# Six small softmax tiles move from a phase's pool to a pool in front of it

## The chip, the cores and the metric

The kernel runs on one core of a Trainium2 chip. The metric is the device time of one execution in microseconds (us). Before the change, three runs gave 1282.92, 1283.75 and 1287.06 us, so the median is 1283.75 us. All inputs and the output are float32.

## The reference: what is computed

Two layers work on 256 latent tokens of width 1024; 256 context tokens go through the first layer's first half as well. Each layer is half-step SwiGLU, token mixer, half-step SwiGLU; the mixer is neighbourhood attention in layer 0 and a short gated convolution in layer 1. Every sub-layer ends in a post-norm update.

```python
def swiglu_ffn(h, w_in, w_out):
    a, u = jnp.split(h @ w_in, 2, axis=-1)          # w_in: 1024 x 5632, w_out: 2816 x 1024
    return (jax.nn.silu(a) * u) @ w_out

def post_norm_update(x, y, gate, res_w, g, b):
    return layer_norm(DN_ALPHA * x + res_w * gate * y, g, b)

x <- post_norm_update(x, f(x * (1 + scale) + shift), gate, w, g, b)   # f: FFN, attention or convolution
```

In the attention each of 16 heads takes a softmax over 256 latent keys (with a bias and a window mask) and 256 context keys. shift, scale and gate come from a product of the conditioning vector with a 1024 x 9216 matrix per layer ("ada").

## The kernel before, in words

**Products.** A float32 product is made of three matmuls on rounded parts: a weight chunk is split into `hi` (ScalarE, L179) and `lo = raw - hi` (VectorE, L182), the activations likewise, and TensorE adds hi by hi, hi by lo and lo by hi into one bank of PSUM (L157, L158, L160 in the helper `mmu`; L549 to L551 in the first FFN, where the weights are the stationary operand and the 512 tokens the moving one). Elsewhere a 128x128 piece of the activations is stationary and 512 columns of the weights are moving. So every such matmul reads two places of SBUF: 128 columns that are loaded as weights, and 512 columns that stream.

**Weight units.** `wunit` (L163 to L183) brings in 128 x 1024 floats (two chunks of 128 rows by 512 columns) by DMA into a `raw` tile and splits it into an `hi` and an `lo` tile. Of these, most come from the pool `wp` (five `hi` and five `lo` buffers). Some come from the pool `hp` of the phase that is running:

```python
        if ext[0] and ext[1] % (5 + ext[0]) in (E0 if ext[0] == 1 else E2):
            hi = hp.tile([P, UN], F32R, tag="whx", bufs=ext[0], name=nm(s + "h"))
            lo = hp.tile([P, UN], F32R, tag="wlx", bufs=ext[0], name=nm(s + "l"))
        else:
            hi = wp.tile([P, UN], F32R, tag="wh", bufs=WB[1], name=nm(s + "h"))
```

In the first phase that is every sixth unit (11 in all, with one extra buffer), in the second phase none, and in the third phase three of every eight (87 in all, with three extra buffers). A unit in the third phase serves 12 matmuls: two tiles of 128 tokens, two chunks, three matmuls. The 11 of the first phase serve 24 each.

**Phases and pools.** SBUF is given out in the order in which pools are opened: `cp` (constants), `wp` (weights), `ap` (38 activation tiles), `sp` (small tiles and scratch), and behind them the pool of the running phase. `ph0` lives through the context tokens' FFN and the latent one's, `ph1` through the attention, `ph2` through the rest; each starts where `sp` ends. `ph0` and `ph2` hold, beside the extra weight buffers, the ada rows (`ar`), their accumulators (`acc`), a few rows more, and in `ph0` the context tokens (`xc`). `ph1` holds `bias` and `kr`, then the six `mx` tiles, then `pr`, `pT` and `oT`.

**Order.** The order on TensorE is written out by hand (a manual schedule, which the helpers `panels`, `tile_panel` and `out_gemm` walk through); a scheduler orders the other engines by priorities. `panels` goes through an FFN's first product in panels of 512 columns: 4 units, 48 matmuls; four units' worth of steps after a panel is done, TensorE transposes its gated result with 8 short matmuls (L408), so a stretch of 48 large matmuls lies between two groups of transposes.

**The softmax.** `scores` (L812 to L834) makes two heads' scores in two PSUM banks, adds the bias, takes the row maximum into `mx[:, 0:1]`, the exponentials with their sum into `mx[:, 1:2]`, and the reciprocal into `mx[:, 2:3]`.

Of the kernel before, what the change touches and what calls it, by code (L numbers as in the profile page):

```python
# [9 lines left out]
F32 = mybir.dt.float32  # L10
# [6 lines left out]
P = 128  # L17
# [48 lines left out]
def backbone_kernel(  # L66
# [11 lines left out]
    sp = ctx.enter_context(tc.tile_pool(name="sp", bufs=2))  # L78
# [3 lines left out]
    hp = phase.__enter__()  # L82
# [6 lines left out]
    def nm(s):  # L89
        uid[0] += 1  # L90
        return f"{s}_{uid[0]}"
# [4 lines left out]
    def bank(tag, s):  # L96
        return pp.tile([P, 512], F32, tag=tag, bufs=PB[tag], name=nm(s))
# [714 lines left out]
    def scores(h, qt):  # L812

        ch = h % 8 // 2
        qh, ql = Q[h // 8].get()[ch // 2]
        qs = slice((ch % 2) * 256 + qt * P, (ch % 2) * 256 + (qt + 1) * P)
        kh, kl = KV[h // 4][0].get()[(h % 4) // 2]
        banks = [bank("at", "S") for _ in range(2)]
        for f in range(3):
            for i in range(2):  # L820
                ps = slice(64 * i, 64 * i + 64)
                nc.tensor.matmul(banks[i], (qh, qh, ql)[f][ps, qs], (kh, kl, kh)[f][ps, :], start=f == 0, stop=f == 2)
        res = []
        for i, S in enumerate(banks):
            Sv = S[:, 0:256].rearrange("p (a b) -> p a b", a=4)
            nc.vector.tensor_tensor(out=Sv, in0=Sv, in1=BIAS.pop((h + i, qt)), op=ALU.add)
            mx = hp.tile([P, 3], F32, tag="mx", bufs=6, name=nm("mx"))
            nc.vector.tensor_reduce(out=mx[:, 0:1], in_=S, axis=AX.X, op=ALU.max, negate=True)
            pr = hp.tile([P, 512], F32, tag="pr", bufs=4, name=nm("pr"))
            nc.scalar.activation(pr, S, AF.Exp, bias=mx[:, 0:1], accum_out=mx[:, 1:2])  # L830
            nc.vector.reciprocal(mx[:, 2:3], mx[:, 1:2])
            nc.scalar.activation(pr, pr, AF.Copy, scale=mx[:, 2:3])
            res.append(pr)
        return res  # L834
# [39 lines left out]
    hp = phase.__enter__()  # L874
# [35 lines left out]
    for i in range(len(steps) + LAG + V_LAG):  # L910
        if i == NX_AT:
            new_x(0, 0, s2t)
            for t in range(2):
                for h in range(2):
                    sync.dma_start(xscr[t * P:(t + 1) * P, h * 512:(h + 1) * 512], xt[t][h])
        while i + AHEAD < len(steps) and len(KV) <= steps[i + AHEAD][0] // 4:
            fill_some(1)
        if i < len(steps) and i % 2 == 0:
            with tc.high_priority(offset=S_EARLY):
                prs[i], prs[i + 1] = scores(*steps[i])  # L920
            if i % 2 == 0 and i + 2 < len(steps):
                bias_pair(*steps[i + 2])
        credit += rate[min(i, len(rate) - 1)]
        n = int(credit)
        credit -= n
        if i >= 24 and fin is None:
            run(fill)
            fin = last_filler()
            fill = islice(fin, 9)
        fill_some((n + 1) // 2)  # L930
        if 0 <= i - LAG < len(steps):
            with tc.high_priority(offset=P_EARLY):
                probs_T(*steps[i - LAG], prs.pop(i - LAG))
        fill_some(n // 2)
        j = i - LAG - V_LAG
        if j >= 0 and steps[j][1] == 1:
            with tc.high_priority(offset=V_EARLY):
                values(steps[j][0])
# [5 lines left out]
    hp = phase.__enter__()  # L944
# [126 lines left out]
```

## Time and profile before

| what | value |
|---|---|
| median of three runs | 1283.75 us |
| the profiled execution's own time | 1283.45 us |
| its span, from first to last instruction | 1281.7 us |
| mean granted TensorE clock | 0.997 |
| TensorE (PE) busy | 1255.1 us, 98% |
| weight loads (PEld) busy | 1005.4 us, 78% |
| VectorE (DVE) busy | 954.6 us, 74% |
| ScalarE (ACT) busy | 591.2 us, 46% |
| DMA | 268.59 MB, mean 210 GB/s |

The page names each group of instructions by its line, its engine and its tiles (`w<-w1h,hTh` is a matmul that writes `w` from the tiles `w1h` and `hTh`). A matmul's listed duration covers the part of its run that overlaps the next one, so durations of matmuls add up to more than the time; how fast TensorE goes is read from the distance between the starts of two matmuls that follow each other. In a table by windows the columns are: the stretch, its length, the engine's busy time in it with the count of instructions that reach into it in brackets, the granted clock, the DMA engines' busy share, GB/s.

### The profile page before, as it was taken

The numbers are of one execution on the slowest core, as the hardware profiler recorded it, in microseconds if no ns is written. First come the engines' busy times: TensorE is split into PE (matmuls) and PEld (weight loads), VectorE is DVE, ScalarE is ACT, GpSimd is POOL, SyncE is SP. The second block draws the span as 40 slices with busy tenths as digits, with TensorE's granted clock in tenths as the row PEclk, the third lists the DMA queues.
The fourth block names the chain that finished last, engine by engine and source line by source line (L and its number), as shares of the span: only waits on it lengthen the run. The fifth ranks groups of instructions, "written<-read, shape, count | busy, mean of one in ns | idle before, by whom it ended". The sixth has DMA issues, their size and how long they took to land.

```text
span 1281.7 us, 17190 instructions
## 1 busy us (share of the span) xinstructions
PE 1255.1 (98%) x5890; PEld 1005.4 (78%) x5890; DVE 954.6 (74%) x1683; ACT 591.2 (46%) x1148; POOL 42.7 (3%) x71
## 2 busy tenths in 40 slices
PE   7999999999999999988999999999999999999997
PEld 4787778788778777766787787887788877788886
DVE  3699878495658777788998788867778787865545
ACT  2432132413236456686556435655435744655431
POOL 0000000000001111120000000000000000000000
PEclk9999999999999999999999999999999999999999
DMA  9977569394622744464999887777886754776641
GB/s 291 301 232 238 181 194 307 123 306 133 204 71 83 216 91 91 92 149 133 307 336 313 307 289 271 233 225 228 290 285 221 247 194 131 226 220 188 229 154 51
DMA packets 202713, 268.59 MB, mean 210 GB/s; under 512 B 30027, under 2 KB 149299, under 8 KB 202625
## 3 DMA queue, kind: packets, MB, share of 16 engines
q1 hardware_dynamic: 202624, 267.49, 65.8%
q8 instruction: 46, 0.75, 0.2%
q14 instruction: 43, 0.34, 0.1%
HBM read 265.27 MB, written 2.17 MB: 209 GB/s over the span
## 4 chain that ended last, share of the span: by engine, by line
PE 87%; DVE 5%; DMA 3%; ACT 3%; issue 1%; POOL 0%; SPq 0%; DVEq 0%; ACTq 0%
PE w L157 16%; PE w L158 16%; PE w L160 16%; PE f L549 6%; PE f L550 6%; PE f L551 6%; PE wkv L157 2%; DMA w1r<-in_ffn_w_in_dram 2%; PE wkv L158 2%; PE wkv L160 2%; PE wc L157 2%; PE wc L158 2%; PE wc L160 2%; DMA ar<-in_ada_w_dram 2%; PE gT L408 1%
## 5 line engine op out<-in xcount | busy, mean ns | idle before, releaser
L179 ACT ACTIVATE w1h<-w1r 128x512 fp32r<-128x512 f32 x352 | 202.6, 625 | 181.4 <-PE w L160 68.8
L182 DVE TENSOR_TENSOR w1l<-w1r,w1h 128x512 fp32r<-128x512 f32 x352 | 227.8, 687 | 65.9 <-ACT w1h L179 63.5
L157 PE MATMUL w<-w1h,hTh 128*128 128x512 f32 x528 | 210.8, 399 | 1.4 <-ACT hTh L106 1.4
L248 DVE SCALAR_TENSOR_TENSOR acc<-ar,cst,acc 128x512 f32<-128x512 f32 x266 | 187.5, 749 | 29.4 <-DMA ar<-in_ada_w_dram 29.4
L158 PE MATMUL w<-w1l,hTh 128*128 128x512 f32 x528 | 207.0, 392 | 0.0
L157 PE MATMUL w<-w2h,gh 128*128 128x512 f32 (+1 forms) x446 | 175.4, 394 | 0.0
L158 PE MATMUL w<-w2l,gh 128*128 128x512 f32 (+1 forms) x446 | 173.6, 390 | 0.0
L179 ACT ACTIVATE w2h<-w2r 128x512 fp32r<-128x512 f32 x176 | 101.5, 624 | 140.2 <-PE w L160 129.4
L160 PE MATMUL w<-w1h,hTl 128*128 128x512 f32 x528 | 163.5, 391 | 0.7 <-DVE hTl L107 0.6
L182 DVE TENSOR_TENSOR w2l<-w2r,w2h 128x512 fp32r<-128x512 f32 x176 | 114.2, 688 | 43.9 <-ACT w2h L179 42.6
L549 PE MATMUL f<-h0h,w1h 128*128 128x512 f32 x352 | 139.6, 396 | 0.4 <-ACT w1h L179 0.4
L551 PE MATMUL f<-h0l,w1h 128*128 128x512 f32 x352 | 138.2, 393 | 0.0
L550 PE MATMUL f<-h0h,w1l 128*128 128x512 f32 x352 | 138.2, 393 | 0.0
L160 PE MATMUL w<-w2h,gl 128*128 128x512 f32 (+1 forms) x446 | 136.3, 387 | 0.0
L157 PEld LDWEIGHTS w<-w1h,hTh 128*128 128x128 f32 x528 | 99.2, 188 | 25.4 <-ACT hTh L106 2.7
L160 PEld LDWEIGHTS w<-w1h,hTl 128*128 128x128 f32 x528 | 98.9, 188 | 24.2 <-DVE hTl L107 1.9
L158 PEld LDWEIGHTS w<-w1l,hTh 128*128 128x128 f32 x528 | 99.2, 188 | 20.4 <-DVE w1l L182 0.3
L157 PEld LDWEIGHTS w<-w2h,gh 128*128 128x128 f32 x446 | 83.8, 188 | 21.7 <-issue 1.7
L160 PEld LDWEIGHTS w<-w2h,gl 128*128 128x128 f32 x446 | 83.3, 188 | 18.8
L158 PEld LDWEIGHTS w<-w2l,gh 128*128 128x128 f32 x446 | 83.7, 188 | 18.0 <-DVE w2l L182 0.7
L549 PEld LDWEIGHTS f<-h0h,w1h 128*128 128x128 f32 x352 | 66.4, 189 | 18.3 <-issue 3.8
L551 PEld LDWEIGHTS f<-h0l,w1h 128*128 128x128 f32 x352 | 66.3, 188 | 14.7 <-DVE h0l L527 0.3
(178 smaller groups left out, 1703.1 us busy)
## 6 DMA issues: line engine op xcount, KB each, us to landing
w1r<-in_ffn_w_in_dram SPq DMA_DIRECT2D x352, 256.0 KB
ar<-in_ada_w_dram SPq DMA_DIRECT2D x128, 512.0 KB
w2r<-in_ffn_w_out_dram SPq DMA_DIRECT2D x88, 512.0 KB
ar<-in_ada_w_dram SPq DMA_DIRECT2D x32, 256.0 KB
wkvr<-in_na_w_qkv_dram SPq DMA_DIRECT2D x32, 256.0 KB
wcr<-in_sc_w_in_dram SPq DMA_DIRECT2D x32, 256.0 KB
wqr<-in_na_w_qkv_dram SPq DMA_DIRECT2D x8, 512.0 KB
bias<-in_na_rpb_dram SPq DMA_DIRECT2D x64, 64.0 KB
```

The lines of the kernel that those rows point to most:

```text
L157: nc.tensor.matmul(ps, lh, rh, start=first and i == 0, stop=False)
L158: nc.tensor.matmul(ps, lh, rl, start=False, stop=False)
L160: nc.tensor.matmul(ps, ll, rh, start=False, stop=last and i == n - 1)
L179: nc.scalar.activation(hi[:, a:a + m // W_HI], raw[:, a:a + m // W_HI], AF.Copy)
L182: nc.vector.tensor_tensor(out=lo[:, a:b], in0=raw[:, a:b], in1=hi[:, a:b].bitcast(F32), op=ALU.subtract)
L248: nc.vector.scalar_tensor_tensor(out=a, in0=src, scalar=sc, in1=a, op0=ALU.mult, op1=ALU.add)
L408: nc.tensor.transpose(ps[:, j * 256 + i * P:j * 256 + (i + 1) * P], g[:, j * P:(j + 1) * P], ident)
L549: nc.tensor.matmul(ps, lh, hT0[k][0], start=(k == 0), stop=False)
L550: nc.tensor.matmul(ps, ll, hT0[k][0], start=False, stop=False)
L551: nc.tensor.matmul(ps, lh, hT0[k][1], start=False, stop=(k == KC - 1))
```

## The change

The six `mx` tiles (128 x 3 floats, 32 bytes of each partition apiece, 192 bytes together) are taken from `sp` and no longer from the phase's pool.

```diff
@@ -824,7 +824,7 @@
         for i, S in enumerate(banks):
             Sv = S[:, 0:256].rearrange("p (a b) -> p a b", a=4)
             nc.vector.tensor_tensor(out=Sv, in0=Sv, in1=BIAS.pop((h + i, qt)), op=ALU.add)
-            mx = hp.tile([P, 3], F32, tag="mx", bufs=6, name=nm("mx"))
+            mx = sp.tile([P, 3], F32, tag="mx", bufs=6, name=nm("mx"))
             nc.vector.tensor_reduce(out=mx[:, 0:1], in_=S, axis=AX.X, op=ALU.max, negate=True)
             pr = hp.tile([P, 512], F32, tag="pr", bufs=4, name=nm("pr"))
             nc.scalar.activation(pr, S, AF.Exp, bias=mx[:, 0:1], accum_out=mx[:, 1:2])
```

The two built programs hold the same instructions in the same order on every engine, with the same semaphores and the same waits. They differ in the addresses of 458 tiles and in nothing else. These are the byte addresses within a partition of the tiles that matter here, and what is left of them when divided by 512:

| tiles | before: address, remainder | after: address, remainder |
|---|---|---|
| weight units in `wp` (`hi`, `lo`) | 38208 + n x 4096 and 58688 + n x 4096: 320 | the same |
| activations in `ap` (38 tiles of 2048) | 79168 + n x 2048: 320 | the same |
| scratch of 2048 in `sp` | 156992 + n x 2048: 320 | the same |
| `mx`, six tiles of 32 | 192128 to 192288 | 179840 to 180000 |
| weight units in `ph0` | 216704, 220800: 128 | 216896, 220992: 320 |
| weight units in `ph2` | 179840 + n x 4096, 192128 + n x 4096: 128 | 180032 + n x 4096, 192320 + n x 4096: 320 |
| `ar`, `acc`, rows, `xc`, gates in `ph0` and `ph2` | remainder 128 | remainder 320 |
| `bias`, `kr` in `ph1` (ahead of `mx`) | remainder 128 | remainder 320 |
| `pr`, `pT`, `oT` in `ph1` (behind `mx`) | 192320 to 229176: 320 | the same |

A chunk within a tile starts a multiple of 512 bytes further on, so each tile keeps one remainder throughout.

## The prediction

> **What bounds the kernel now.** I read the page's busy times and chain of waits first.
>
> ```profile
> PE 1255.1 (98%) x5890; PEld 1005.4 (78%) x5890; DVE 954.6 (74%) x1683; ACT 591.2 (46%) x1148; POOL 42.7 (3%) x71
> ...
> PE 87%; DVE 5%; DMA 3%; ACT 3%; issue 1%; POOL 0%; SPq 0%; DVEq 0%; ACTq 0%
> ```
>
> TensorE sets the end, so any nanosecond per matmul counts some 4,900 times. The next view is that of the waits, of TensorE and then of ScalarE.
>
> ```profile
> PE ada L502 <- DMA ar<-in_ada_w_dram: 5.0, 5, 1.6
> ...
> PE w L157 <- ACT hTh L106: 1.4, 3, 0.6
> ...
> PE f L549 <- ACT w1h L179: 0.4, 1, 0.4
> ...
> ACT w2h L179 <- PE w L160: 129.4, 59, 17.3
> ...
> ACT w1h L179 <- PE w L160: 68.8, 50, 16.7
> ...
> ACT w1h L179 <- DMA w1r<-in_ffn_w_in_dram: 51.7, 34, 5.5
> ```
>
> TensorE waits for nothing for long (5.0 us is its longest entry, all at the start). ScalarE, which makes the weights' `hi` tiles, waits 198 us for TensorE to free a buffer and 52 us for weights to land: the supply is ahead.
>
> So the question is how fast TensorE goes where it waits for nothing. That is read from the starts in the timeline of PE. Here is a stretch of the first FFN; the first six matmuls use a unit of `wp`, the six from 193.87 on the one unit of `ph0`, those after 195.27 units of `wp` again (the program's order tells which).
>
> ```profile
> 192.51 0.39 PE L549 MATMUL f<-h0h,w1h 128*128 128x512 f32 x1
> 192.74 0.39 PE L550 MATMUL f<-h0h,w1l 128*128 128x512 f32 x1
> ...
> 193.87 0.40 PE L549 MATMUL f<-h0h,w1h 128*128 128x512 f32 x1
> 194.10 0.39 PE L550 MATMUL f<-h0h,w1l 128*128 128x512 f32 x1
> 194.34 0.40 PE L551 MATMUL f<-h0l,w1h 128*128 128x512 f32 x1
> ...
> 195.27 0.39 PE L549 MATMUL f<-h0h,w1h 128*128 128x512 f32 x1
> ...
> 196.66 0.39 PE L549 MATMUL f<-h0h,w1h 128*128 128x512 f32 x1
> ```
>
> From 192.51 to 193.87 are six steps: 1.36 us, 226.7 ns each. From 193.87 to 195.27, with the phase's unit: 1.40 us, 233 ns. From 195.27 to 196.66, back on `wp`: 1.39 us, 232 ns. Nothing waits; TensorE is simply slower while one of its operands lies in a tile of remainder 128, and for about six matmuls after it.
>
> The same shows in whole panels of the last FFN. Of every eight units three lie in `ph2`; the transposes cut these so that in one stretch 5 of 47 matmuls use them and in the next 30.
>
> ```profile
> 1114.30:1124.76 10.46, 10.46 (x47) 1.00 0.51 156
> 1125.66:1136.26 10.60, 10.60 (x47) 1.00 0.77 244
> 1137.17:1147.63 10.46, 10.46 (x47) 1.00 0.57 176
> 1148.53:1159.13 10.60, 10.60 (x48) 1.00 0.58 177
> 1160.03:1170.51 10.48, 10.48 (x48) 1.00 0.58 175
> 1171.41:1182.01 10.60, 10.60 (x48) 1.00 0.59 174
> ```
>
> Each window holds 46 steps. 10.46 us is 227.4 ns a step, 10.60 is 230.4 ns. The clock is full in all six and the DMA share 0.57 to 0.59 in four of them, so neither makes the difference; 25 matmuls more on phase tiles cost 0.14 us.
>
> **Is it the remainder, or the place high up in SBUF?** The attention's output product answers: there the stationary operand `oT` lies at 217408 to 228672, as high as the phase's weight units, but behind `mx` and so at remainder 320.
>
> ```profile
> 592.63 0.39 PE L157 MATMUL wo<-woh,oT 128*128 128x512 f32 x1
> ...
> 593.53 0.39 PE L157 MATMUL wo<-woh,oT 128*128 128x512 f32 x1
> ...
> 596.71 0.39 PE L157 MATMUL wo<-woh,oT 128*128 128x512 f32 x1
> ```
>
> At 593.53 the stationary operand goes from `ap` (146752) to `ph1` (217408). The 18 steps from 592.63 to 596.71 take 4.08 us, 226.7 ns each, with no break at the crossing. Distance in SBUF costs nothing; what the slow steps share is two operands of different remainder.
>
> **The change part by part.** Nothing is added or removed, and the order of instructions is the same on every engine, so there is no new wait to cost. Three things change their address.
>
> *The weight units of the phases*, 98 units, 1,308 matmuls (87 x 12 and 11 x 24), go to remainder 320, that of all other operands of the large matmuls. I took the windows of all 43 stretches of at least 37 large matmuls without a break.
>
> ```profile
> 49.10:99.50 50.40, 50.40 (x222) 1.00 0.79 249
> ...
> 612.73:621.94 9.21, 9.21 (x41) 1.00 0.92 313
> ...
> 701.32:711.92 10.60, 10.60 (x47) 1.00 1.06 383
> ...
> 1217.19:1269.19 52.00, 52.00 (x228) 1.00 0.33 109
> sum 818.60, PE 818.60; mean PE 19.04
> ```
>
> They hold 3,573 steps (a window's steps are its count less one, or the count where its edge trims one) and 1,004 of the 1,308 matmuls. At 226.7 ns the steps would take 809.9 us; 8.7 us are over. Not all of this goes: after every break TensorE needs some ten steps to fall into 226.7 ns even on `wp` alone. In the 10.46 us panels that and 5 phase matmuls cost 0.03 us over 46 x 226.7 ns = 10.43. I leave 0.03 x 43 = 1.3 us of it and take 7.4 us, 7.4 ns for each of the 1,004 matmuls. The other 304 lie in short stretches between transposes that are mostly settling anyway; I take half, 304 x 3.7 = 1.1 us (bounds 0 and 2.6, the latter at the full 8.7/1,004). Together 8.5 us.
>
> What could swallow it is the supply. In the windows from 612.73 to 711.92 the DMA engines are at 0.86 to 1.06; the nine stretches there have 0.7 us of the 7.4. I take off half, 0.4: 8.1 us.
>
> *The other phase tiles* (`ar`, `acc`, `bias`, `kr`, `xc`) are read and written by VectorE, DMA and short transposes. For VectorE the trace has the same operation on both remainders, `xc` in `ph0` and `x` in `ap`:
>
> ```profile
> L313 DVE TENSOR_TENSOR xc<-xc,res 128x512 f32<-128x512 f32 x8 | 5.5, 692 | 0.2
> L313 DVE TENSOR_TENSOR x<-x,res 128x512 f32<-128x512 f32 x8 | 5.5, 691 | 0.1
> ...
> L315 DVE SCALAR_TENSOR_TENSOR xc<-xc,res 128x512 f32<-128x512 f32 x4 | 2.8, 688 | 0.0
> ```
>
> 692 against 691 ns: nothing, under TensorE besides. *The `mx` tiles* stay in buffers of their own, six as before, in the same order: nothing.
>
> The profiled execution's 1283.45 us (span 1281.7 and 1.75 around it) less 8.1 is 1275.3; the median of the runs is 0.3 above that execution, so the forecast is **1275.6 us**.
>
> **The rivals.**
>
> *No effect (1283.7 us).* The units of the phases could be slow for another reason than their remainder. For it: no moving operand of 512 columns ever lies that high at remainder 320; `oT` above is a stationary one. Against it: in the first FFN the phase's unit is the stationary operand, exactly `oT`'s role, at about `oT`'s place, and there it is slow. The Trainium skill, "SBUF — State Buffer", section "Who interferes with whom", speaks for this rival: TensorE has two independent read ports, one for the moving operand and one for weight loads, and PE and ACT never wait on anyone. By that rule no address could matter; the rows of the panels above (10.46 and 10.60 us on the same work) disagree with it.
>
> *Half (1279.7 us).* The new phase units lie at 832 beyond a multiple of 1024, those of `wp` at 320. If the step depends on more of the moving operand's address than the remainder by 512, each unit keeps its break. Against it: stationary chunks alternate between the two in every tile without harm (the 226.7 ns stretches do). Half of 8.1 is 4.05 us, off the median of 1283.75.
>
> *The supply becomes the bound (1280.8 us).* Nine stretches with DMA shares near 1 lie in the third phase; if all that phase's gain turned into waits for weights, only the 2.9 us of the eight windows before 600 us (same working) would stay. Against it are ScalarE's 198 us of waiting for TensorE.
>
> *Slower (1291 us).* The new relation could be the bad one. The slowest steps in the trace without a wait are these:
>
> ```profile
> 577.04:578.22 1.18, 1.18 (x6) 1.00 0.07 14
> ```
>
> Five steps in 1.18 us, 236 ns, unsettled, both operands at remainder 320 and behind transposes. Were the 1,308 matmuls to run at that and not at the panels' 230.4 ns, 7.3 us would be added. It decides against me once they are over 230.4 + 3.85/1,308 = 233.3 ns. Against it: 320 with 320 is where all the 226.7 ns steps are.
>
> **How the numbers follow.** Chances: the forecast 0.77, half 0.06, supply 0.04, no effect 0.10, slower 0.03. About 0.3%, 3.85 us, is what a measurement of this kernel can tell from no change, so faster means below 1279.9. Faster holds the forecast and most of half: 0.82; within 0.3% holds no effect, the supply case and the rest: 0.15; slower 0.03. The range: at the low end the settling goes too and the short stretches give their upper bound, 8.7 + 2.6 = 11.3 us, 1272.4; the high end takes in half and the supply case, 1281. That leaves out 0.13.
>
> **What would show it.** In the profile after: the last FFN's stretches all take about 10.46 us; six steps on a phase's unit in the first FFN take 1.36 us and the six behind them too; the mean of L158's and L551's matmuls falls by 1 to 3 ns; the 43 stretches sum to about 811 us; TensorE's waits stay as they are; L179's and L182's means do not move. The forecast is wrong if the stretches with 30 phase matmuls still take 10.60 us (no effect), if they fall and ScalarE's waits for DMA grow by as much (supply), or if they exceed 10.73 us (slower: 46 x 233.3).

## The result, and the profile after

The median of six runs of the changed kernel is 1277.55 us (1277.28 to 1279.28); six runs of the kernel before give 1284.72 us (1282.92 to 1287.06). The ratio is 0.9946, with a 95% interval of 0.9933 to 0.9959: a gain of 7.2 us, and 5.3 to 8.6 us by the interval. The forecast was 1275.6 us. The profiled execution took 1277.28 us (span 1275.5), 6.2 us less than the one before.

The page's busy times, its chain, and the groups that answer to the question of the supply (after):

```profile
PE 1247.6 (98%) x5890; PEld 1005.4 (79%) x5890; DVE 954.5 (75%) x1683; ACT 590.3 (46%) x1148; POOL 41.9 (3%) x71
...
PE 74%; DVE 10%; DMA 9%; ACT 3%; issue 2%; SPq 1%; POOL 0%; DVEq 0%; ACTq 0%
...
L179 ACT ACTIVATE w1h<-w1r 128x512 fp32r<-128x512 f32 x352 | 202.6, 625 | 182.5 <-PE w L160 68.2
...
L158 PE MATMUL w<-w1l,hTh 128*128 128x512 f32 x528 | 205.9, 390 | 0.0
...
L551 PE MATMUL f<-h0l,w1h 128*128 128x512 f32 x352 | 137.8, 391 | 0.0
```

The same groups in the page of before:

```profile
L179 ACT ACTIVATE w1h<-w1r 128x512 fp32r<-128x512 f32 x352 | 202.6, 625 | 181.4 <-PE w L160 68.8
...
L158 PE MATMUL w<-w1l,hTh 128*128 128x512 f32 x528 | 207.0, 392 | 0.0
...
L551 PE MATMUL f<-h0l,w1h 128*128 128x512 f32 x352 | 138.2, 393 | 0.0
```

TensorE is busy for 7.5 us less, VectorE and ScalarE within 0.9 us of before; a matmul of L158 or L551 lasts 2 ns less. TensorE's share of the chain falls from 87 to 74%, and VectorE and DMA take its place. This looks like a supply that has come closer to the end, but the share is no measure of it: it is 84% in the repeat of this kernel, and 84% as well in the kernel that has the slow steps back (both below).

The stretch of the first FFN with the phase's unit, in the timeline of PE (after); the unit of `ph0` serves the six matmuls from 193.33 on:

```profile
191.97 0.39 PE L549 MATMUL f<-h0h,w1h 128*128 128x512 f32 x1
...
193.33 0.39 PE L549 MATMUL f<-h0h,w1h 128*128 128x512 f32 x1
...
194.69 0.39 PE L549 MATMUL f<-h0h,w1h 128*128 128x512 f32 x1
...
196.05 0.39 PE L549 MATMUL f<-h0h,w1h 128*128 128x512 f32 x1
```

Each time six steps take 1.36 us, 226.7 ns a step: the 1.40 and 1.39 us of before are gone. The panels of the last FFN, windows (after):

```profile
1120.85:1131.30 10.45, 10.45 (x47) 1.00 0.78 247
1132.20:1142.66 10.46, 10.46 (x48) 1.00 0.63 186
1143.56:1154.01 10.45, 10.45 (x48) 1.00 0.57 178
1154.91:1165.36 10.45, 10.45 (x47) 1.00 0.58 177
```

The change between 10.46 and 10.60 us is gone too; every panel is at 10.45 or 10.46. All stretches of at least 36 large matmuls without a break (after), first and last row of the windows:

```profile
49.77:99.66 49.89, 49.89 (x221) 1.00 0.79 248
...
sum 813.49, PE 813.49; mean PE 18.49
```

There are 44 of them with 3,583 steps. At 226.7 ns these would take 812.1 us, so 1.35 us is over, where 8.7 us was over before. Over all 4,902 large matmuls, counting the steps under 245 ns (the others hold a wait or a break), the sum above 226.67 ns falls from 12.51 to 4.12 us: **8.4 us of steps are saved**.

Only half of that was lost on the phase units' own matmuls. On the steps that are counted in both executions, 3.3 us are saved on 1,119 steps where a phase unit is the moving operand (2.9 ns each), 0.9 us on 142 where it is the stationary one (6.5 ns each), and 4.2 us on the first ten steps behind each of 123 returns to a unit of `wp` (some 34 ns a return), where both operands lie well. From the eleventh step behind a return on nothing is saved.

The profiled execution gained 6.2 us only. So 2.2 us came back elsewhere. TensorE's waits (after) show part of it:

```profile
PE ada L502 <- DMA ar<-in_ada_w_dram: 5.4, 5, 1.8
...
PE w L157 <- ACT hTh L106: 1.2, 3, 0.6
...
PE gT L408 <- DVE sil L400: 0.6, 2, 0.3
...
PE w L158 <- DVE w2l L182: 0.2, 1, 0.2
```

The last two are not in the list of before: twice the transposes wait for VectorE's `sil`, and once a matmul waits for a `lo` tile. (Both kinds come up again below in kernels whose steps are as slow as before.) The first of them in the timeline of PE (after), in brackets the wait and what ended it:

```profile
662.97 0.44 PE L408 MATMUL gT<-ident,sil 128*128 128x128 f32 x2 [0.27 <-DVE sil L400]
```

Matched matmul by matmul, the two executions differ by 0.4 to 0.6 us at each of these three places, and by 0.7 us in the first 30 us, where TensorE waits for transfers.

### The profile page after: what moved, and what is told of

Read it like the earlier page. It is cut to its first block, busy times and chain, and to the rows that moved or that the text cites. A ratio compares the mean times of both kernels' runs of the same rounds, so it can differ in the third digit from the quotient of the medians.

```text
span 1275.5 us, 17190 instructions
## 1 busy us (share of the span) xinstructions
PE 1247.6 (98%) x5890; PEld 1005.4 (79%) x5890; DVE 954.5 (75%) x1683; ACT 590.3 (46%) x1148; POOL 41.9 (3%) x71
## 4 chain that ended last, share of the span: by engine, by line
PE 74%; DVE 10%; DMA 9%; ACT 3%; issue 2%; SPq 1%; POOL 0%; DVEq 0%; ACTq 0%
PE w L157 12%; PE w L160 12%; PE w L158 12%; PE f L549 6%; PE f L550 6%; PE f L551 6%; DMA ar<-in_ada_w_dram 4%; DMA w1r<-in_ffn_w_in_dram 3%; DVE w1l L182 3%; PE wkv L157 2%; PE wkv L160 2%; PE wkv L158 2%; PE wc L157 2%; PE wc L160 2%; PE wc L158 2%
## 5 line engine op out<-in xcount | busy, mean ns | idle before, releaser
L179 ACT ACTIVATE w1h<-w1r 128x512 fp32r<-128x512 f32 x352 | 202.6, 625 | 182.5 <-PE w L160 68.2
L182 DVE TENSOR_TENSOR w1l<-w1r,w1h 128x512 fp32r<-128x512 f32 x352 | 227.4, 685 | 62.8 <-ACT w1h L179 60.5
L158 PE MATMUL w<-w1l,hTh 128*128 128x512 f32 x528 | 205.9, 390 | 0.0
L158 PE MATMUL w<-w2l,gh 128*128 128x512 f32 (+1 forms) x446 | 172.4, 387 | 0.2 <-DVE w2l L182 0.2
L179 ACT ACTIVATE w2h<-w2r 128x512 fp32r<-128x512 f32 x176 | 101.5, 624 | 139.7 <-PE w L160 127.9
L182 DVE TENSOR_TENSOR w2l<-w2r,w2h 128x512 fp32r<-128x512 f32 x176 | 114.0, 687 | 42.9 <-ACT w2h L179 41.8
L551 PE MATMUL f<-h0l,w1h 128*128 128x512 f32 x352 | 137.8, 391 | 0.0
L158 PEld LDWEIGHTS w<-w1l,hTh 128*128 128x128 f32 x528 | 99.2, 188 | 19.7 <-DVE w1l L182 0.3
L158 PEld LDWEIGHTS w<-w2l,gh 128*128 128x128 f32 x446 | 83.8, 188 | 17.6 <-DVE w2l L182 1.1
L551 PEld LDWEIGHTS f<-h0l,w1h 128*128 128x128 f32 x352 | 66.4, 189 | 14.3 <-DVE h0l L527 0.3
```

Source lines behind the costliest of these rows:

```text
L158: nc.tensor.matmul(ps, lh, rl, start=False, stop=False)
L179: nc.scalar.activation(hi[:, a:a + m // W_HI], raw[:, a:a + m // W_HI], AF.Copy)
L182: nc.vector.tensor_tensor(out=lo[:, a:b], in0=raw[:, a:b], in1=hi[:, a:b].bitcast(F32), op=ALU.subtract)
L551: nc.tensor.matmul(ps, lh, hT0[k][1], start=False, stop=(k == KC - 1))
```

## The experiments

In all ten kernels every engine has the instructions of the changed kernel, in its order and with its waits; only addresses differ. A `pad` or `gap` tile is written and read by nobody. `crow` (16 rows of the conditioning vector, used at the start alone) is moved into a buffer of `mrow` where room was short. Kernels for which no number of runs is given ran once; what is read from them is mainly the steps inside their profiled execution. "Excess" is the sum of the large matmuls' steps above 226.67 ns, counted as above: 12.51 us before, 4.12 us after. The difference that is spoken of is the address of the moving operand less that of the stationary one.

### The remainder alone is put back

```diff
+    hp.tile([P, 80], F32, tag="pad", name="pad0")      # head of ph0, 320 bytes
+    hp.tile([P, 80], F32, tag="pad", name="pad2")      # head of ph2
```

`mx` stays in `sp`; the tiles of `ph0` and `ph2` lie at remainder 128 again.

> The mx tiles stay in sp, but 320 bytes of unused padding at the head of ph0 and ph2 put their tiles back to remainder 128 (crow, used once at the start, lies in a buffer of mrow to make room). Theory 'remainder' (a large matmul steps at 226.7 ns only if its two operands have the same remainder by 512): time as before the change, about 1284.7 us; long stretches of the last FFN alternate between 10.46 and 10.60 us. Rival 'mx' (the gain came from where mx lies, or from ph1): stays at 1277.5 us, all stretches near 10.45 us.

Measured: 1283.55 us (ten runs), ratio to the kernel before 0.9993 (0.998 to 1.0006), excess 12.56 us. Three panels of the last FFN, windows:

```profile
1128.16:1138.74 10.58, 10.58 (x47) 1.00 0.82 253
1139.64:1150.12 10.48, 10.48 (x47) 1.00 0.59 173
1151.03:1161.63 10.60, 10.60 (x48) 1.00 0.59 186
```

The two kinds of panel are back, and with them the whole time. Where the `mx` tiles lie does nothing; the remainder of the phases' tiles does it all.

### Other offsets: 64, 128, 256 and 32 bytes

```diff
+    hp.tile([P, 16], F32, tag="pad", name="pad0")      # 64 bytes; 128, 256 and 32 with P x 32, 64 and 8
+    hp.tile([P, 16], F32, tag="pad", name="pad2")
```

> The changed kernel with ph0 and ph2 64 bytes further on: their tiles at remainder 384, all others at 320. Theory 'remainder by 512': slow as before, 1284 us, stretches with 30 phase matmuls 10.60 us. Rival 'any period of 64 bytes or less' is already out by the 192 bytes of the change itself; rival 'only place or distance matters': 1277.5 us, 10.45 us.

> ph0 and ph2 128 bytes further on: remainder 448 against 320. Theory 'remainder by 512': slow, 1284 us, stretches 10.60 us. Rival 'the period is 128 bytes' (192 is not a multiple of 128, so the first kernel's slowness fits it too): 1277.5 us and 10.45 us.

> ph0 and ph2 256 bytes further on: remainder 64 against 320 (crow in a buffer of mrow, for room). Theory 'remainder by 512': slow, 1284 us, stretches 10.60 us. Rival 'the period is 128 or 256 bytes': 1277.5 us and 10.45 us.

> The changed kernel with ph0 and ph2 32 bytes further on: remainder 96 by 256 against 64. The moving operand is 32 bytes ahead of the stationary one in the third phase, 32 behind in the first FFN. Theory 'whole address lines of 64 bytes or more decide': 32 bytes lie in part in the same line; steps between 226.7 and 229 ns, 1277.5 to 1280 us. Rival 'each byte of difference costs' (64 bytes: 229 to 230.4 ns, 192 the other way: 233): third phase about 228.5 ns, first FFN's unit over 230 ns, 1281 to 1284 us. A third outcome, under 226.7 ns, would be a better relation than equal remainders.

Measured: 64 bytes 1285.41 us, excess 12.61; 128 bytes 1288.98 us, excess 12.80; 256 bytes **1277.97 us, excess 4.15**; 32 bytes 1284.86 us, excess 14.42. The kernel before gave 1284.42 us beside the first three and 1283.84 us beside the last. Panels of the last FFN, one fence for each kernel (64, 128, 256, 32):

```profile
1127.61:1138.21 10.60, 10.60 (x47) 1.00 0.78 239
1139.12:1149.58 10.46, 10.46 (x47) 1.00 0.59 176
```

```profile
588.30:595.10 6.80, 6.29 (x19) 0.51 0.20 67
...
1142.52:1152.98 10.46, 10.46 (x48) 1.00 0.59 177
1153.88:1164.54 10.66, 10.66 (x47) 1.00 0.59 183
```

```profile
1132.83:1143.28 10.45, 10.45 (x48) 1.00 0.61 178
1144.18:1154.65 10.47, 10.47 (x47) 1.00 0.59 179
```

```profile
1138.06:1148.55 10.49, 10.49 (x48) 1.00 0.58 175
1149.46:1160.14 10.68, 10.68 (x47) 1.00 0.58 175
```

An offset of 256 bytes costs nothing, though the remainder by 512 is then 64 for the phases and 320 for the rest. So the relation repeats every 256 bytes. By 256 the 64-byte kernel has the same two differences as the kernel before (64 and 192), at other addresses, and its excess is that of before to 0.1 us. 32 bytes is no milder than 64 or 128: I had expected only part of the cost, and its panels are the slowest of the four. Of the time at 128 bytes a part is not the offset's: the first row of its fence is a stretch of the attention, 6.8 us long, at a granted clock of 0.51, and the kernel before has full clock at that place. At half clock that is some 3.4 us of work, which would account for most of the 4.6 us over the kernel before.

### The common operands are moved instead

```diff
+    gp = ctx.enter_context(tc.tile_pool(name="gp", bufs=1))
+    gp.tile([P, 80], F32, tag="gap", name="gap")        # between wp and ap
     ap = ctx.enter_context(tc.tile_pool(name="ap", bufs=NACT))
```

Now the units of `wp` stay at remainder 320 and everything behind them, activations and phase units, lies at 128. If the place of the phases' units made the slow steps, this would change nothing; if it is the relation, most matmuls become slow and those on phase units fast.

> 320 bytes of unused room between wp and ap: the weight units of wp stay at remainder 320 by 512, everything behind them (activations, sp, phase tiles) goes to 128, so that now the phase units match the activations and the 230 units of wp do not. Theory 'the two operands of a matmul must agree by 256 bytes': about 3,500 of the 4,902 large matmuls mismatch instead of 1,300; at 230 to 233 ns a step against 227 that is 10 to 20 us over the changed kernel, 1287 to 1297 us, slower than the kernel before. Rival 'tiles of the phase pools have to lie at 320' or 'only the phase tiles matter': as before, 1284.5 us. Rival 'place does not matter once mx is out of the way': 1277.5 us.

Measured: 1289.68 us (before: 1283.47), excess 21.91 us. Three panels of the last FFN, windows:

```profile
1130.58:1141.16 10.58, 10.58 (x47) 1.00 0.73 234
1142.06:1152.79 10.73, 10.73 (x48) 1.00 0.56 170
1153.69:1164.27 10.58, 10.58 (x47) 1.00 0.61 189
```

The kinds of panel have changed places: those with 30 matmuls on phase units are now the faster, and those with 42 on `wp` take 10.73 us. That decides it: no unit is slow in itself, and the two operands' difference makes the step. This kernel also has long settled stretches at two differences in one execution, windows of it, and of before for the steps on `wp` alone and for a run on phase units:

```profile
301.93:322.76 20.83, 20.83 (x93) 1.00 0.27 85
422.79:440.99 18.20, 18.20 (x79) 1.00 0.72 235
```

```profile
300.45:321.08 20.63, 20.63 (x93) 1.00 0.27 89
827.86:830.84 2.98, 2.98 (x15) 1.00 0.10 20
```

20.83 us over 91 steps is 228.9 ns (difference 64 by 256), 18.20 us over 78 steps is 233.3 ns (192), 20.63 us over 91 is 226.7 ns (0); the short run before, 2.98 us over 13, is 229 ns (64). Runs of the same 13 steps at 128 and at 32 bytes:

```profile
831.47:834.51 3.04, 3.04 (x15) 1.00 0.11 18
```

```profile
826.96:829.99 3.03, 3.03 (x15) 1.00 0.10 20
```

| difference by 256 bytes | settled step | over 226.7 |
|---|---|---|
| 0 | 226.7 ns (3,565 steps of the changed kernel) | 0 |
| 32 | 233.1 ns (201 steps) | 6.4 |
| 64 | 228.2 to 229.0 ns (201 steps before, 539 here) | 1.5 to 2.3 |
| 128 | 233.6 ns (202 steps) | 6.9 |
| 192 | 233.3 ns (1,010 steps here) | 6.6 |

These are means over the steps from the eleventh on behind a break or a change of the difference, as long as the next matmul has the same difference; a step more or less at either end moves those for 32, 64 and 128 by up to 1.3 ns. So the kernel before had two prices: where the phase unit is moving the difference is 64, where it is stationary, in the first FFN, 192. The 32-byte kernel has its phase units 32 bytes behind there, a difference of 224: 142 steps, 5.7 ns over on the mean, in groups too short to settle.

### Settling and the identity

Of the 4.12 us of excess that are left, 1.35 lie in the long stretches and 2.8 in the short ones, behind the groups of transposes. Those read the identity, at remainder 128. This kernel puts 320 bytes behind the identity, so that all large operands lie at its remainder:

```diff
     make_identity(nc, ident)
+    cp.tile([P, 80], F32, tag="gap", name="gap")
```

> 320 bytes of unused room behind the identity matrix: all operands of the large matmuls go to remainder 128 by 512, where the identity (the moving operand of all transposes) lies already. Theory 'the ten slow steps after a group of transposes come from the identity's other remainder': the steps' excess over 226.7 ns falls from 4.1 us to about 1 us, 1274 to 1275 us. Rival 'any break of the stream unsettles TensorE': excess stays 4.1 us, 1277.5 us. 'Only 320 settles': 1290 us and more.

Measured: 1277.17 us (five runs), ratio 0.9949 (0.9933 to 0.9966), excess 4.26 us. Two panels, windows:

```profile
1130.71:1141.16 10.45, 10.45 (x47) 1.00 0.59 180
1142.06:1152.53 10.47, 10.47 (x47) 1.00 0.60 176
```

Nothing of it went away: my idea that the identity's remainder causes the settling fell. So did 'only 320 settles': with all large operands at 128 the panels are as fast as at 320. The first ten steps behind a break are over by 5, 6, 6, 3, 3, 3, 1, 1, 1 and 0 ns, some 30 ns together, with the identity at their remainder as without. That is the price of a break, and a return to a unit of `wp` cost about as much in the kernel before (34 ns).

### Which part of the phases

The changed kernel with the 320 bytes at the head of `ph2` alone:

```diff
     hp = phase.__enter__()
+    hp.tile([P, 80], F32, tag="pad", name="pad2")       # ph2 only
```

> Padding of 320 bytes in ph2 alone: ph0 stays at 320, ph2 goes back to 128. Theory: the steps' excess of the first phase stays away (3 us), that of the third returns (5.4 us of 8.4): 1282 to 1283 us, the stretches of the last FFN alternate between 10.46 and 10.60 us, the six steps on the phase's unit in the first FFN take 1.36 us. Rival 'the third phase's gain is given back as waits for weights': 1277.5 us.

Measured: 1281.39 us (before: 1283.47), excess 9.61 us; its panels in the last FFN are those of before:

```profile
1123.60:1134.20 10.60, 10.60 (x48) 1.00 0.70 217
1135.11:1145.57 10.46, 10.46 (x48) 1.00 0.57 174
```

12.51 - 9.61 = 2.9 us comes from `ph0`'s 264 matmuls and 5.5 us from `ph2`'s 1,044, each with the steps behind them. The last experiment leaves only the weight units of `ph2` at remainder 320 and puts `ar`, `acc` and the rows there back to 128:

```diff
+    if not odd and ext[0] == 3: odd.append(hp.tile([P, 80], F32, tag="pad", name="pad2"))
     w = hp.tile([P, D], F32, tag="ar", bufs=3, name=nm("ar"))
```

> The changed kernel with 320 bytes of padding in ph2 between the weight units and the ada rows: weight units at remainder 320, ar, acc and the bias rows back at 128 in the third phase (crow in a buffer of mrow, for room). Theory 'only the large matmuls' operands matter': as the changed kernel, 1277.5 us, steps' excess 4.1 us, L248's mean unchanged within 3 ns of 746. Rival 'VectorE or the ada transfers gain too': L248 back at 749 or more and 1278.5 us or more with unchanged steps.

Measured: 1278.30 us (before: 1283.84), excess 4.10 us. A panel, and the ada product's operation on VectorE (count, then minimum, median and maximum in ns), the second row from the view by line:

```profile
1133.12:1143.57 10.45, 10.45 (x47) 1.00 0.60 181
...
L248 DVE SCALAR_TENSOR_TENSOR acc<-ar,cst,acc x266: 733/746/754, 64.9 to 968.2; 128x512 f32<-128x512 f32 x133
```

In the third phase the weight units' remainder alone gives all of the gain. The row's median is 746 ns in the changed kernel and 749 ns before. Here 112 of its 266 operations are back at 128, and their mean is 746.8 ns against 746.7 in the changed kernel; with all of them at 128, in the kernel with the gap behind the identity, the median is 745. So these 3 ns are not their address.

### The changed kernel once more

> The changed kernel again, beside the one with the identity in line. Both theories: 1277.5 us, ratio 0.9946 to the kernel before.

Measured: 1277.39 us (ten runs, 1275.24 to 1283.22), ratio 0.9958 (0.9944 to 0.9973), excess 4.08 us. This time the profiled execution took 1275.24 us, and only 0.2 us of the 8.4 came back. Its list of TensorE's waits has no `gT` and no `w2l`; two of its entries are:

```profile
PE ada L502 <- DMA ar<-in_ada_w_dram: 4.9, 4, 1.5
...
PE hT L343 <- DVE x L335: 1.1, 2, 0.9
```

Both are found with slow steps too: TensorE's waits in the 32-byte kernel, then in the 64-byte one (its lines are numbered one higher):

```profile
PE gT L408 <- DVE sil L400: 0.6, 2, 0.3
```

```profile
PE w L159 <- DVE w2l L183: 0.5, 1, 0.5
...
PE gT L409 <- DVE sil L401: 0.3, 1, 0.3
```

The chain of the repeat and, for comparison, that of the kernel with the remainder put back, which has the slow steps:

```profile
PE 84%; DVE 5%; DMA 5%; ACT 3%; issue 1%; SPq 1%; POOL 0%; DVEq 0%; ACTq 0%
```

```profile
PE 84%; DVE 5%; DMA 5%; ACT 3%; issue 1%; SPq 0%; POOL 0%; DVEq 0%; ACTq 0%
```

Five profiled executions have difference 0 in all large matmuls: the changed kernel's two, and those with 256 bytes, with the gap behind the identity and with the weight units alone. In all five the steps take 8.3 to 8.4 us less than before. What came back in other gaps was 2.2, 0.2, 2.7, 0.7 and 3.2 us (the time from the first matmul to the last, against that of before less the steps' gain). But this part varies with slow steps as well: the time from the first matmul to the last less the excess is 1258.5 to 1261.5 us in these five, and 1257.7 to 1260.8 in five with phase units out of line (before, put back, 64, 32 and `ph2` alone). Only the kernel with the common operands moved, with the slowest steps, stands clearly lower, at 1255.0 (the 128-byte one, with its half clock, is at 1263.6).

## Why the prediction was right, and where it was off

**What bounds the kernel.** Right: TensorE. It is 98% busy before and after, and taking nanoseconds from its steps gave 7.2 us by the medians.

**Remainder, not place.** Right, and now shown and not only argued: putting the remainder back takes the whole gain away (ratio 0.9993), and moving the common operands makes the phase's matmuls the fast ones. The reading of `oT` at 593.53 us, an operand high in SBUF with no break, held.

**The remainder by 512.** This is the step that was too coarse. It is the remainder by 256, and the difference between the two operands: 256 bytes of offset cost nothing (4.15 us of excess), and 32 bytes cost about as much a settled step as 128 (233.1 and 233.6 ns). It made no difference here, since 320 and 832 agree by either rule. The prediction's 233 ns on a phase unit in the first FFN was a difference of 192, and the milder cost of the panels one of 64. The trace of before had shown these two, and I took a single mean over them, 7.4 ns a phase matmul. It is the price of no settled matmul: these cost 1.5 to 2.3 or 6.6 ns, and half of the sum lay on the ten steps behind each return. I had seen these ("for about six matmuls after it") and had them in the sum of the stretches without naming them. The sum held because it was taken over whole stretches; another division into units would likely have had another mean. (Of the 1,308 matmuls 12 have 256 columns and are not in the 4,902; 1,296 are.)

**The sum of the long stretches.** 7.4 us was forecast; 8.7 - 1.35 = 7.4 us is measured. At the 3,573 steps of before, 227.04 ns a step give 811.2 us, against the "about 811". The 0.03 us of settling that I left in each stretch is 1.35/44 = 0.03; I had taken it from the 10.46 us panels alone, which have 5 phase matmuls, so that it fits all stretches is in part luck.

**The short stretches.** 1.1 us was forecast, 8.4 - 7.4 = 1.0 us is measured. The half that I took was a guess between 0 and 2.6, so this is luck.

**The other phase tiles and `mx`: nothing.** Right by the kernels that move one and not the other: with `mx` in `sp` and the remainder put back the time is that of before; with `ar` and `acc` at 128 the gain stays. L179's means did not move (625 and 624 ns), L182's by 2 and 1 ns.

**What the supply takes, 0.4 us.** This is the term with the least behind it. I looked for it inside the nine stretches where the DMA engines are full (the last of the nine ends at 723.29, not 711.92, and their DMA shares go from 0.77 to 1.06). There it took nothing: these stretches' excess fell from 1.00 to 0.26 us, all of the 0.7 us that they held. In the first profiled execution 2.2 us came back at other places: at `gT` behind VectorE's `sil`, at a `lo` tile, and in the first 30 us. "TensorE's waits stay as they are" was wrong there, and nearly right in the repeat (0.2 us). But the same waits at `gT` and at a `lo` tile stand in kernels with slow steps, and the kernel with the remainder put back has the steps of before to 0.05 us and still ended 2.5 us later in its profiled execution than the one before. So these gaps come and go with TensorE at either speed, and that they are the change's is not shown.

The median is 1.95 us above the forecast. Of this 1.0 us is the starting point: the kernel before has 1284.72 us over six runs, and the forecast set out from the 1283.75 of three. The gain is 7.2 us where 8.15 was forecast, and the interval (5.3 to 8.6) holds both; in the repeat it is 6.1 us by the medians and 3.5 to 7.2 by the interval. So of the 8.4 us of steps 1.2 and 2.3 us did not show in the medians, more than the 0.4. Whether a faster TensorE is what lengthens the other gaps stays open; the 1255.0 us of the kernel with the slowest steps would fit it, one execution.

**The rivals.** *No effect* fell with the panels of 10.45 us. The rule that stood behind it, from the Trainium skill, "SBUF — State Buffer", section "Who interferes with whom" (separate read ports for moving operand and weight load, PE never waits), read as "no address can matter", does not hold here: 226.7 against 233.3 ns a step at full clock, by the two addresses alone. *Half* fell too: units at 832 run beside those at 320 without a break, and 256 bytes made no difference. *The supply becomes the bound* did not come about as put: ScalarE's wait for the transfers of the FFNs' first weights fell instead of growing, from 51.7 to 45.8 us (after, a row of ScalarE's waits). The fall is not the change's either: with the remainder put back it is 46.0.

```profile
ACT w1h L179 <- DMA w1r<-in_ffn_w_in_dram: 45.8, 31, 4.9
```

*Slower* fell for this change. Its mechanism, a bad relation that becomes the common one, is real: the kernel with the common operands moved is it, at 1289.68 us, with 2,583 steps at a mean of 233.35 ns. The 233.3 ns from which it was to decide happens to be the settled price of a difference of 192.

## What to carry to other kernels

Where matmuls on fp32 parts follow each other with a weight load each and nothing waits, compare the distance of their starts between groups that differ only in where an operand lies; a few ns a step that no list of waits shows is 0.5% of the time here. Then look at the two operands' addresses by 256 bytes and put all pools of such operands at the same remainder; one pad tile, or a small tile moved out of a phase's pool, does it. Count the steps behind each return to a well-placed operand too: here they were half of the loss, so the number of changes matters beside the number of matmuls. And look for a wait that is new after a change in runs that have its effect undone, before it is called the change's price: here the wait at `gT` (0.6 us) is there too, with 0.4 us.

## What was not expected of the hardware

- The step of these matmuls depends on the difference of the two operands' addresses by 256 bytes: 226.7 ns at 0, 228.2 to 229.0 at 64, and 233.1 to 233.6 at 32, 128 and 192. At 224 only groups of six were seen, 5.7 ns over; other differences were not tried, and why the two addresses matter to each other no run shows.
- 32 bytes costs three to four times what 64 bytes costs (6.4 ns a step against 1.5 to 2.3).
- Behind a group of transposes the first ten steps are some 30 ns over in all, whether the identity lies at the operands' remainder or not. A return from a difference of 64 or 192 to 0, with no break in the stream, costs about as much (34 ns).
- No arrangement went under 226.7 ns, and none of the ten kernels is faster than the changed one by more than the runs can tell (the identity's, at 1277.17 us beside its 1277.39, is equal).
